# Side steps of a first MLP map tied to the emptying of a PSUM bank

## The chip, the cores and the metric

The kernel runs on one core of a Trainium2 chip, in one launch. The metric is device time in microseconds (us) from start to end of the execution. The engines are TensorE (PE for matmuls, PEld for its weight loads), VectorE (DVE), ScalarE (ACT), GpSimd (POOL) and SyncE (SP); each works through its own instructions in a fixed order and waits on semaphores for the others. DMA transfers are issued from the queues of SP and POOL.

## What is computed

One decoder layer over 2048 tokens of width 1024, in float32. `c` modulates both halves.

```python
mod = (silu(c) @ w_ada + b_ada)[:, None, :]
sh1, sc1, g1, sh2, sc2, g2 = jnp.split(mod, 6, axis=-1)
h = x * (1.0 + sc1) + sh1
z = h @ w_in                              # 1024 -> 2048
gate_b, gate_c, v_conv, v_pool = jnp.split(z, [512, 1024, 1536], axis=-1)
y_conv = gate_b * _short_conv(gate_c * v_conv, conv_w)
y_pool = _multiscale_pool(v_pool, w_pool, pool_scale)
mix = jnp.concatenate([y_conv, y_pool], axis=-1) @ w_out
x = _layer_norm(ALPHA * x + (1.0 + g1) * mix, ln1_g, ln1_b)
h = x * (1.0 + sc2) + sh2
f = jnp.square(jax.nn.relu(h @ w_mlp_in)) @ w_mlp_out   # 1024 -> 4096 -> 1024
x = _layer_norm(ALPHA * x + (1.0 + g2) * f, ln2_g, ln2_b)
```

## The kernel before

Every float32 operand of a matmul is split into a high part (an ACT copy, L135) and a low part (a DVE subtraction, L136; both in `split`), and a product is made of three matmuls (`mm3`, L140 to L142: high x high, high x low, low x high). The large maps use a scheme of seven block products in place of eight (as Strassen and Winograd have it), so sums and differences of blocks of the weights and of the activations are needed; most are made by DVE (`tt`, L145), stored to DRAM by POOL and loaded again by SP.

The tokens are worked in two blocks `b` of 1024. For each, `first_map` makes the first MLP map (1024 to 4096) in eight groups `up(b, g, ...)` of 512 columns. A group is seven products from `seven`, each of 24 matmuls into two PSUM banks. The weights of a product come from one of two generators. `summed_weights` loads blocks and sums ready from DRAM (block 1, and the first two groups of block 0; L599). `block_weights` (groups 2 to 7 of block 0) loads four blocks (L567), makes the sums on DVE (tiles `r`, L145), and stores them for block 1 (L577). Pools bound how far ahead this runs: `w` holds six tiles (three products of a high and a low part), `r` five, `o` is shared by results and side work.

After a product its two banks are emptied: by `keep` (two ACT copies, L1039), by `add` in `join` (two DVE adds, L145) or, for the last product of a group, by two ACT Relus (L1124). Relu and square of the joined results follow on ACT (L1051, L1052, L1125), and `sums` makes the block sums of the results for the second map (DVE L145, POOL stores L1064).

Beside the products, `beside` takes one step of a generator of side work, once the first groups are through: 48 steps in each block. In block 0 it is `first_side`: four steps of modulation vectors (loads L265), steps of `sum_down`, four steps `sum_x` (loads of xT at L647, an ACT affine at L648, DVE sums), two halves of `sum_weights` (loads L587), and more of `sum_down`. In block 1 it is `sum_down` alone; what is left of it runs in the second map. A step of `sum_down` makes up to two sums of blocks of the second map's weights on DVE (128x512), stores them by POOL (L1140) and issues up to three loads for the steps after it on SP (L1142), into halves of three tiles that are used over and over. So a load waits until its half has been read or stored, and an add of a later step waits for the load.

A scheduler orders the instructions of each engine by their dependencies and by priorities that follow the order in the program. Before, the dictionary `mark` held the latest weight split or bank add on DVE and the latest weight load on SP, and `beside` let every instruction of a step on those engines stand behind them, as an order within the same engine, with no wait for another engine:

```python
def beside():
    if open_:
        with tc.issue_after(mark["DVE"]), tc.issue_after(mark["SP"]):
            next(side, None)
```

Of the kernel before, what the change touches and what calls it, by code (L numbers as in the profile page):

```python
# [1 line left out]

# [8 lines left out]
AF = mybir.ActivationFunctionType  # L11
ALU = mybir.AluOpType
# [85 lines left out]
def tile_hybrid_layer(ctx: ExitStack, tc: tile.TileContext, opening, xT, x, wada, win,  # L98
                      wins, wpool, wout, wmix, w1, w2, rows, out):
    nc = tc.nc  # L100
# [11 lines left out]
    def mk(p, shape, dt, tag, bufs):  # L112
        names[0] += 1
        return p.tile(shape, dt, name=f"{tag}_{names[0]}", tag=tag, bufs=bufs)
# [7 lines left out]
    def t_w(dt=F32R):  # L122
        return mk(big, [P, T], dt, "w", 6)
# [10 lines left out]
    def split(src, hi, lo):  # L134
        high = nc.scalar.copy(hi, src)  # L135
        return high.ins, nc.vector.tensor_tensor(lo, src, hi.bitcast(F32), op=ALU.subtract).ins  # L136
# [7 lines left out]
    def tt(out_, a, b_, op):  # L144
        return nc.vector.tensor_tensor(out_, a, b_, op=op)  # L145
# [54 lines left out]
    def row_of(dst, cols):  # L200
        banks = spread(cols)
        for h, hs in enumerate(halves):
            nc.scalar.copy(dst[:, hs], banks[h])
# [58 lines left out]
    def ada(f0, f1, load=nc.gpsimd.dma_start, tiles=lambda: t_h(F32)):  # L262
        for f in range(f0, f1):
            r = tiles()
            load(r, wada[f - G1])  # L265
            dot(f, r)
        biased(f0, f1)
# [61 lines left out]
    def parts(src, t=t_h):  # L329
        hi, lo = t(), t()  # L330
        split(src, hi, lo)
        return hi, lo
# [207 lines left out]
    def beside(j, m, g1):  # L540
        for what in plan.get((j, m), "").split():
            n = int(what[1:])
            if what[0] == "r":
                ada(n, n + 2)
            elif what[0] == "f":
                fold(n, g1)
            elif what[0] == "b":
                row_of(g1, mod[:, G1 : G1 + KD])
            elif what[0] == "l":
                fold_weights(n)  # L550
            elif what[0] == "g":
                gated(n // 2, n % 2, g1)
            elif what[0] == "s":
                sum_out(n, t_o)
            else:
                sum_weights(w1[n], w1sum[n], t_o)

    mark = {}  # L560
    RAW = range(4)
    ORDER = (("11", "11"), ("12", "21"), ("s2", "2"), ("s1", "1"), ("s3", "3"), ("s4", "22"), ("22", "4"))

    def block_weights(src, dst=None):
        a11, a12, a21, a22 = [t_r() for _ in range(4)]
        for i, r in enumerate((a11, a12, a21, a22)):
            mark["SP"] = nc.sync.dma_start(r, src[i]).ins  # L567
        yield a11
        yield a12
        s1 = t_r()  # L570
        tt(s1, a21, a22, ALU.add)
        tt(a21, a11, a21, ALU.subtract)
        tt(a11, s1, a11, ALU.subtract)
        tt(a12, a12, a11, ALU.subtract)
        if dst is not None:
            for i, r in enumerate((s1, a11, a21, a12)):
                nc.gpsimd.dma_start(dst[i], r)  # L577
        for r in (a11, s1, a21, a12, a22):
            yield r
# [16 lines left out]
    def summed_weights(src, sums, order):  # L596
        for i in order:
            r = t_r()
            mark["SP"] = nc.sync.dma_start(r, src[i] if i in RAW else sums[i - 4]).ins  # L599
            yield r  # L600

    def seven(ready, B, first_w=None):
        made = [first_w] if first_w else []

        def product(i, banks, new):
            if made:
                hi, lo = made.pop()
            else:
                r = next(ready)
                hi, lo = t_w(), t_w()  # L610
                mark["DVE"] = split(r, hi, lo)[1]
            for p in range(2):
                if new:
                    banks[p] = t_ps()
                for k in range(4):
                    bh, bl = B[ORDER[i][1], k // 2]
                    ks = slice((k % 2) * H, (k % 2) * H + H)
                    cs = slice(p * H + k * P, p * H + k * P + P)
                    mm3(banks[p], hi[:, cs], lo[:, cs], bh[:, ks], bl[:, ks], new and k == 0, k == 3,
                        not new)  # L620

        return product
# [403 lines left out]
    def sum_out(g, tiles):  # L1026
        sum_blocks([gout[i % 2, i // 2 * 2 + g] for i in range(4)], wosum[g], tiles)

    def up(b, g, B, beside, turn):
        X, Y, Z = {}, {}, {}  # L1030
        order = (0, 1, 5, 4, 6, 7, 3) if g else (0, 1, 7, 4, 5, 6, 3)
        product = seven(summed_weights(w1[g], w1sum[g], order) if b or g < 2 else block_weights(w1[g], w1sum[g]), B)
        ps = [slice(p * H, p * H + H) for p in range(2)]
        parts_, where, spare = {}, {}, []

        def keep(banks):
            r = t_o()
            for p in range(2):
                nc.scalar.copy(r[:, ps[p]], banks[p])  # L1039
            return r  # L1040

        def add(r, banks):
            for p in range(2):
                mark["DVE"] = tt(r[:, ps[p]], r[:, ps[p]], banks[p], ALU.add).ins

        def join(r, banks):
            add(r, banks)
            squared(r)

        def squared(r):  # L1050
            nc.scalar.activation(r, r, AF.Relu)  # L1051
            nc.scalar.activation(r, r, AF.Square)  # L1052

        def cell(r, i):
            return r[:, i * Q : i * Q + Q]

        def made(r, fh, th):
            for q in range(2):
                for f in range(2):
                    i = 4 * (2 * th + q) + 2 * fh + f  # L1060
                    parts_[i] = where[i] = cell(r, 2 * f + q)

        def stored(slot, z):
            nc.gpsimd.dma_start(usum[slot, g // 2, :, b, g % 2, :], z)  # L1064

        def sums(stage):
            if stage == 0:
                stored(RAW_SLOT[0], parts_[RAW_SLOT[1]])
            for x, y, sign, slot, at in U_SUMS[stage]:
                if at not in parts_:  # L1070
                    r = t_o()
                    parts_.update({16 + 4 * len(spare) + i: cell(r, i) for i in range(4)})
                    spare.append(r)
                z = parts_[at]
                tt(z, where[x], where[y], ALU.add if sign > 0 else ALU.subtract)
                where[16 + sum(k > 15 for k in where)] = z
                if slot >= 0:
                    stored(slot, z)

        product(0, X, True)  # L1080
        c11 = keep(X)
        beside()
        product(1, Y, True)
        join(c11, Y)
        made(c11, 0, 0)
        sums(0)
        beside()
        yield
        if g == 0:
            product(5, Y, True)  # L1090
            yield
            product(3, Z, True)
            c22 = keep(Z)
            yield
        product(2, X, False)
        c12 = keep(X)
        if g == 0:
            add(c12, Y)
            join(c12, Z)
            yield  # L1100
        else:
            beside()
            product(3, Z, True)
            c22 = keep(Z)
            beside()
        product(4, X, False)
        join(c22, X)
        made(c22, 1, 1)
        sums(1)
        beside()  # L1110
        if g == 0:
            yield
        else:
            if g == NC - 1:
                turn()
            product(5, Z, False)
            join(c12, Z)
            beside()
        made(c12, 0, 1)
        sums(2)  # L1120
        product(6, X, False)
        c21 = t_o()
        for p in range(2):
            nc.scalar.activation(c21[:, ps[p]], X[p], AF.Relu)  # L1124
        nc.scalar.activation(c21, c21, AF.Square)  # L1125
        made(c21, 1, 0)
        sums(3)
        beside()


    def sum_down():
# [247 lines left out]
    def first_map(b, B, back):  # L1379
        side = sums_down if b else first_side()  # L1380
        open_ = []

        def beside():
            if open_:
                with tc.issue_after(mark["DVE"]), tc.issue_after(mark["SP"]):
                    next(side, None)

        def turn():
            if b + 1 < NB:
                ready.append(prepare())  # L1390

        ups = [up(b, g, B, beside, turn) for g in range(NC)]
        for g in range(2):
            next(ups[g])
            back(1 + g)
        for i in range(3, 7):
            next(ups[0])
            back(i)
        open_.append(True)
        for g in range(NC):  # L1400
            for _ in ups[g]:
                pass

    ready = []
# [60 lines left out]
```

## Time and profile before

| what | value |
|---|---|
| median of 3 runs | 1855.06 us (1849.86 to 1859.36) |
| the profiled execution | 1847.54 us, its span 1845.5 us |
| PE, DVE, ACT, POOL busy | 1723.2, 1416.8, 842.6, 402.4 us |
| mean granted TensorE clock | 0.969 |
| DMA | 478.95 MB, mean 260 GB/s |

The profile shows one execution. Its groups of instructions name the line, the engine, the operation and the tiles (output <- inputs). A wait is put down to what ended it. In the timeline a row has its start, its duration, and in brackets the idle time just before it with what released it. The first map of block 0 with its side steps lies at about 380 to 660 us of the span, that of block 1 at about 945 to 1250 us.

### The profile page before, as it was taken

Reading aid. Unit: us, or ns where it says so; the run is one execution under the profiler, and the core shown is the slowest. Engines: PE = TensorE matmul, PEld = TensorE weight load, DVE = VectorE, ACT = ScalarE, POOL = GpSimd, SP = SyncE. Lnnn points to the kernel's source line nnn. Section 1 sums busy time; section 2 is a strip of 40 time slices with the busy share of each in tenths; the row PEclk is TensorE's granted clock in tenths of the full one; section 3 lists DMA queues with packets and bytes.
Section 4 is the critical chain, followed back from the end, with each engine's and each line's share of the span. In section 5 each row is a group of like instructions: output and inputs, shape, how many; then the busy total and the mean of one; then the engine's idle time right before and its main releaser. Section 6 shows DMA issues by size and latency. Waiting matters only on the chain.

```text
span 1845.5 us, 22577 instructions
## 1 busy us (share of the span) xinstructions
PE 1723.2 (93%) x7519; PEld 1414.0 (77%) x7519; DVE 1416.8 (77%) x2222; ACT 842.6 (46%) x1148; POOL 402.4 (22%) x767
## 2 busy tenths in 40 slices
PE   9999998777969789999988999998999999999998
PEld 8888886656747678888866877876888888888887
DVE  7997886687777776689676787777675586686998
ACT  6322475344434374344754444454544334353552
POOL 0223121244454430010113455443000000000000
PEclk9999999888989999999998999999999999999999
DMA  9998764588987874257546888889977787666772
GB/s 388 349 338 321 301 247 161 189 289 283 327 290 278 285 249 151 98 189 261 181 162 224 283 291 292 292 281 353 370 273 250 254 285 284 221 246 219 268 277 80
DMA packets 155205, 478.95 MB, mean 260 GB/s; under 512 B 22600, under 2 KB 23120, under 8 KB 155088
## 3 DMA queue, kind: packets, MB, share of 16 engines
q1 hardware_dynamic: 100960, 304.44, 47.8%
q0 software_dynamic: 54128, 173.07, 26.0%
q8 instruction: 59, 0.97, 0.2%
q14 instruction: 58, 0.48, 0.1%
HBM read 315.40 MB, written 162.01 MB: 259 GB/s over the span
## 4 chain that ended last, share of the span: by engine, by line
PE 48%; DMA 10%; DVE 9%; issue 5%; POOL 2%; ACT 1%; SPq 0%; DVEq 0%; POOLq 0%; ACTq 0%
PE ps L142 16%; PE ps L141 16%; PE ps L140 16%; DVE o L145 6%; DMA o<-in_w 3%; DMA wsum<-o 3%; DMA usum<-o 2%; DVE w L136 2%; POOL usum L1064 1%; DMA r<-in_w 1%; DMA r<-winsum 1%; DVE h L136 0%; DMA o<-hsave 0%; DMA o<-in_xT 0%; POOL wsum L1140 0%
## 5 line engine op out<-in xcount | busy, mean ns | idle before, releaser
L140 PE MATMUL ps<-h,w 128*128 128x512 f32 x1312 | 522.4, 399 | 61.9 <-ACT w L135 39.1
L142 PE MATMUL ps<-h,w 128*128 128x512 f32 x1312 | 521.5, 399 | 34.3 <-DVE w L136 34.2
L141 PE MATMUL ps<-h,w 128*128 128x512 f32 x1312 | 521.2, 397 | 9.3 <-DVE h L136 9.3
L141 PE MATMUL ps<-h,h 128*128 128x512 f32 (+1 forms) x1064 | 413.3, 388 | 6.2 <-DVE h L136 6.2
L142 PE MATMUL ps<-h,h 128*128 128x512 f32 (+1 forms) x1064 | 413.2, 388 | 0.0
L140 PE MATMUL ps<-h,h 128*128 128x512 f32 (+1 forms) x1064 | 412.3, 388 | 0.0
L140 PEld LDWEIGHTS ps<-h,w 128*128 128x128 f32 x1312 | 252.4, 193 | 119.6 <-ACT w L135 41.2
L142 PEld LDWEIGHTS ps<-h,w 128*128 128x128 f32 x1312 | 252.7, 193 | 94.2 <-DVE w L136 41.4
L145 DVE TENSOR_TENSOR o<-o,o 128x256 f32<-128x256 f32 (+2 forms) x554 | 265.6, 527 | 55.0 <-DMA o<-in_w 23.1
L141 PEld LDWEIGHTS ps<-h,w 128*128 128x128 f32 x1312 | 252.9, 193 | 65.7 <-DVE h L136 12.0
L1064 POOL DMA_DIRECT2D usum<-o x416 | 222.9, 541 | 232.6 <-DVE o L145 173.3
L135 ACT CAST w<-r 128x1024 fp32r<-128x1024 f32 x156 | 163.5, 1051 | 228.5 <-PE ps L141 210.1
L135 ACT CAST h<-r 128x1024 fp32r<-128x1024 f32 (+1 forms) x144 | 144.8, 1011 | 235.5 <-PE ps L141 121.0
L141 PEld LDWEIGHTS ps<-h,h 128*128 128x128 f32 x1064 | 200.3, 188 | 48.0 <-DVE h L136 7.1
L136 DVE TENSOR_TENSOR w<-r,w 128x1024 fp32r<-128x1024 f32 x156 | 190.4, 1223 | 58.7 <-ACT w L135 58.3
L140 PEld LDWEIGHTS ps<-h,h 128*128 128x128 f32 x1064 | 200.1, 188 | 41.2 <-DVE o L944 0.2
L142 PEld LDWEIGHTS ps<-h,h 128*128 128x128 f32 x1064 | 200.2, 188 | 40.8
L136 DVE TENSOR_TENSOR h<-r,h 128x1024 fp32r<-128x1024 f32 (+1 forms) x144 | 167.6, 1171 | 64.4 <-ACT h L135 64.0
L145 DVE TENSOR_TENSOR o<-o 128x256 f32<-128x256 f32 (+1 forms) x240 | 125.3, 530 | 73.9 <-DMA o<-in_w 48.5
L145 DVE TENSOR_TENSOR o<-o,ps 128x512 f32<-128x512 f32 x172 | 113.8, 685 | 30.0 <-PE ps L142 27.8
L136 DVE TENSOR_TENSOR h<-w,h 128x1024 fp32r<-128x1024 f32 x104 | 127.0, 1221 | 6.9 <-ACT h L135 6.8
L135 ACT CAST h<-w 128x1024 fp32r<-128x1024 f32 x104 | 108.8, 1046 | 18.2 <-DVE w L145 9.7
(163 smaller groups left out, 1350.2 us busy)
## 6 DMA issues: line engine op xcount, KB each, us to landing
usum<-o POOLq DMA_DIRECT2D x416, 128.0 KB, 4.8
r<-usum SPq DMA_DIRECT2D x104, 512.0 KB, 5.2
wsum<-o POOLq DMA_DIRECT2D x136, 256.0 KB, 4.9
w<-wsum SPq DMA_DIRECT2D x68, 512.0 KB, 5.3
r<-in_w SPq DMA_DIRECT2D x54, 512.0 KB, 5.6
o<-in_w SPq DMA_DIRECT2D x104, 256.0 KB, 4.9
r<-w1sum SPq DMA_DIRECT2D x40, 512.0 KB, 5.3
w<-in_w SPq DMA_DIRECT2D x36, 512.0 KB, 6.1
```

Of the source, the lines that this page charges most:

```text
L135: high = nc.scalar.copy(hi, src)
L136: return high.ins, nc.vector.tensor_tensor(lo, src, hi.bitcast(F32), op=ALU.subtract).ins
L140: nc.tensor.matmul(ps, whi, xhi, start=first, stop=False, skip_group_check=goes_on)
L141: nc.tensor.matmul(ps, whi, xlo, start=False, stop=False, skip_group_check=goes_on)
L142: nc.tensor.matmul(ps, wlo, xhi, start=False, stop=last, skip_group_check=goes_on)
L145: return nc.vector.tensor_tensor(out_, a, b_, op=op)
L1064: nc.gpsimd.dma_start(usum[slot, g // 2, :, b, g % 2, :], z)
```

## The change

Each product now leaves in `mark` the instruction that empties its second bank: the ACT copy of `keep`, the DVE add of `add`, or the ACT Relu of the last product. `beside` gets this instruction, and `behind` adds to every DVE and SP instruction that the step traces a dependency on it. On the same engine it is an order; across engines it is a wait on a semaphore. So a load on SP always waits for ACT or DVE, and an add on DVE waits for ACT after a `keep` or a Relu. Instructions of a step on ACT and POOL get no such dependency. The old marks go: a step no longer has to stand behind the latest weight split on DVE or the latest weight load on SP. The steps, their loads and their sums are the same.

```diff
-    mark = {}
+    @contextmanager
+    def behind(ins):
+        traced = nc.cur_bb.bb.instructions
+        n = len(traced)
+        yield
+        for i in traced[n:]:
+            if i.engine in (nc.vector.engine, nc.sync.engine):
+                tc.add_manual_dep(i, ins.name, mybir.DependencyInfo(
+                    mybir.DependencyClass.NoSync if i.engine == ins.engine else mybir.DependencyClass.Sync,
+                    mybir.DependencyReason.DATA), reason="behind")
...
-            mark["SP"] = nc.sync.dma_start(r, src[i]).ins
+            nc.sync.dma_start(r, src[i])
...
-            if made:
-                hi, lo = made.pop()
-            else:
-                r = next(ready)
-                hi, lo = t_w(), t_w()
-                mark["DVE"] = split(r, hi, lo)[1]
+            hi, lo = made.pop() if made else parts(next(ready), t_w)
...
     def up(b, g, B, beside, turn):
-        X, Y, Z = {}, {}, {}
+        X, Y, Z, mark = {}, {}, {}, [None]
...
         def keep(banks):
             r = t_o()
             for p in range(2):
-                nc.scalar.copy(r[:, ps[p]], banks[p])
+                mark[0] = nc.scalar.copy(r[:, ps[p]], banks[p]).ins
             return r
 
         def add(r, banks):
             for p in range(2):
-                mark["DVE"] = tt(r[:, ps[p]], r[:, ps[p]], banks[p], ALU.add).ins
+                mark[0] = tt(r[:, ps[p]], r[:, ps[p]], banks[p], ALU.add).ins
...
-        beside()
+        beside(mark[0])
...
         for p in range(2):
-            nc.scalar.activation(c21[:, ps[p]], X[p], AF.Relu)
+            mark[0] = nc.scalar.activation(c21[:, ps[p]], X[p], AF.Relu).ins
...
-        def beside():
+        def beside(ins):
             if open_:
-                with tc.issue_after(mark["DVE"]), tc.issue_after(mark["SP"]):
+                with behind(ins):
                     next(side, None)
```

All seven calls of `beside` in `up` are changed in this way, and `summed_weights` like `block_weights`. `parts`, which was there already, makes the two tiles, splits into them and returns them.

More of the change, by code (lines that the diff above doesn't have):

```diff
@@ L1 @@
-from contextlib import ExitStack, nullcontext
+from contextlib import ExitStack, contextmanager, nullcontext
 import concourse.bass as bass
@@ L598, in summed_weights @@
             r = t_r()
-            mark["SP"] = nc.sync.dma_start(r, src[i] if i in RAW else sums[i - 4]).ins
+            nc.sync.dma_start(r, src[i] if i in RAW else sums[i - 4])
             yield r
@@ L1086, in up @@
         sums(0)
-        beside()
+        beside(mark[0])
         yield
@@ L1101, in up @@
         else:
-            beside()
+            beside(mark[0])
             product(3, Z, True)
             c22 = keep(Z)
-            beside()
+            beside(mark[0])
         product(4, X, False)
@@ L1109, in up @@
         sums(1)
-        beside()
+        beside(mark[0])
         if g == 0:
@@ L1117, in up @@
             join(c12, Z)
-            beside()
+            beside(mark[0])
         made(c12, 0, 1)
@@ L1127, in up @@
         sums(3)
-        beside()
+        beside(mark[0])
     def sum_down():
```

## The prediction

> **What bounds the kernel now.** I read the page first, for the engine that sets the time.
>
> ```profile
> span 1845.5 us, 22577 instructions
> PE 1723.2 (93%) x7519; PEld 1414.0 (77%) x7519; DVE 1416.8 (77%) x2222; ACT 842.6 (46%) x1148; POOL 402.4 (22%) x767
> ```
>
> PE is busy for 93% of the span. So a gain can only come from its idle stretches, and a loss only from new ones. The change acts in the first MLP map of each token block. The table of stretches puts these two maps at about 380 to 660 us and 945 to 1250 us.
>
> ```profile
> core 0: us, PE busy (x) PEld busy (x) DVE busy (x) ACT busy (x) POOL busy (x), PEclk, DMA share, GB/s
> 380.00:660.00 280.00, 226.26 (x937) 182.80 (x938) 210.47 (x368) 118.12 (x140) 128.49 (x240) 0.90 0.83 288
> 660.00:945.00 285.00, 279.62 (x1253) 230.23 (x1252) 219.92 (x315) 153.21 (x233) 32.73 (x58) 0.99 0.54 188
> 945.00:1250.00 305.00, 279.39 (x1176) 226.45 (x1175) 229.84 (x419) 138.62 (x163) 133.88 (x250) 0.96 0.82 267
> ```
>
> Without side work (660 to 945) PE idles 285 - 279.6 = 5.4 us. In the first map of block 0 it idles 280 - 226.3 = 53.7 us, in that of block 1, 305 - 279.4 = 25.6 us. DVE has 210 of 280 us of work there, and the DMA engines are 82 to 83% busy. The view of waits names what PE waits for (line, what ended the wait, total, times, longest), first for 380 to 660, then for 945 to 1250.
>
> ```profile
> PE ps L140 <- ACT w L135: 38.2, 4, 18.1
> PE ps L142 <- DVE w L136: 18.7, 6, 5.2
> DVE o L145 <- DMA o<-in_w: 22.0, 6, 5.6
> ```
>
> ```profile
> PE ps L142 <- DVE w L136: 11.3, 4, 4.7
> DVE o L145 <- DMA o<-in_w: 37.8, 12, 7.3
> ```
>
> In block 0 PE waits for weights: the high half (ACT cast, L135) or the low half (DVE subtraction, L136). Behind both stand the sums of the weight blocks and the side steps, all on DVE in one fixed order. The side steps themselves wait for loads.
>
> **The change: what is held.** No instruction is added or removed; the costs are those of order and of new waits. Before, a step's DVE adds (L145) and SP loads (L1142, L587, L647) only had to stand behind the latest weight split or bank add, and the latest weight load. After, each waits until the bank of the product beside it is empty. Matched with its bank's emptying (I call that the mark), 73 of 114 side loads and 57 of 174 side adds of the trace started before it; 13 loads more than 10 us before. The others lose nothing. Two such cases, loads of a step at 464 to 467 us and the ends of the bank adds they will wait for (ACT starts right behind these):
>
> ```profile
> 464.05 1.34 SPq L1142 DMA_DIRECT2D o<-in_w  x3
> 465.70 1.63 SPq L647 DMA_DIRECT2D o<-in_xT  x2
> 472.78 1.06 ACT L1051 ACTIVATE o<-o 128x1024 f32<-128x1024 f32 x1 [0.86 <-DVE o L145]
> 478.72 1.06 ACT L1051 ACTIVATE o<-o 128x1024 f32<-128x1024 f32 x1 [1.35 <-DVE o L145]
> ```
>
> The three loads go 472.8 - 464.1 = 8.7 us later, the two of xT 478.7 - 465.7 = 13.0 us. Behind a held load stand on SP the weight loads of the group (L567, L599); behind a held add stand on DVE the bank adds and weight splits, and for these PE waits. POOL's stores of sums follow their adds. A load, once issued, lands as this row says:
>
> ```profile
> o<-in_w SPq DMA_DIRECT2D x104, 256.0 KB, 4.9
> ```
>
> The new order has a second effect, in block 0. The static order shows the four block sums (r<-r,r, L145, 5.00 us) of a group and its first splits standing 27 to 62 places earlier on DVE. Thus weights can be ready earlier.
>
> **Stall by stall.** These are the starts of PE after its long idles, with the idle and its releaser in brackets:
>
> ```profile
> 386.14 0.80 PE L140 MATMUL ps<-h,w 128*128 128x512 f32 x1 [9.25 <-ACT w L135]
> 390.42 0.79 PE L142 MATMUL ps<-h,w 128*128 128x512 f32 x1 [3.48 <-DVE w L136]
> 453.71 0.80 PE L142 MATMUL ps<-h,w 128*128 128x512 f32 x1 [3.00 <-DVE w L136]
> 552.27 0.80 PE L140 MATMUL ps<-h,w 128*128 128x512 f32 x1 [18.12 <-ACT w L135]
> 595.43 0.50 PE L142 MATMUL ps<-h,w 128*128 128x512 f32 x1 [2.39 <-DVE w L136]
> 602.98 0.50 PE L142 MATMUL ps<-h,w 128*128 128x512 f32 x1 [1.81 <-DVE w L136]
> 646.77 0.80 PE L142 MATMUL ps<-h,w 128*128 128x512 f32 x1 [5.24 <-DVE w L136]
> 1030.70 0.50 PE L142 MATMUL ps<-h,w 128*128 128x512 f32 x1 [1.10 <-DVE w L136]
> 1154.36 0.79 PE L142 MATMUL ps<-h,w 128*128 128x512 f32 x1 [4.70 <-DVE w L136]
> 1209.39 0.50 PE L142 MATMUL ps<-h,w 128*128 128x512 f32 x1 [2.95 <-DVE w L136]
> ```
>
> ```profile
> 389.14 1.22 DVE L136 TENSOR_TENSOR w<-r,w 128x1024 fp32r<-128x1024 f32 x1
> 393.29 5.00 DVE L145 TENSOR_TENSOR r<-r,r 128x1024 f32<-128x1024 f32 x4
> ```
>
> At 386 and 390 PE had stood since 386.14 - 9.25 = 376.9. In the new order the split of 389.14 stands 34 places earlier, that of the next product 28, and the four sums lie ahead of the side adds. The 9.25 + 3.48 = 12.7 us go. Late next is the third product: two run from 376.9 to about 387.8 (24 matmuls of about 0.227 us each), and its low half stands behind side adds whose load now waits for the mark and for an add before it, issued near 388.5. It lands 4.9 us later, at 393.4; an add (0.6), a block sum (1.2) and the split (1.2) end near 396.5. A stall of 8.7 us stays: 8.7 - 12.7 = -4.0.
>
> At 453 the block sum moves behind a bank add and a step's xT loads behind their mark; I get a restart near 450.6, or -3.1 in all: +1.0.
>
> At 496 the held loads of the rows at 464.05 and 465.70 feed DVE and the ACT affine (L648), which stands ahead of the next Relu on ACT. I take the rest of the shift as given back: +3.1.
>
> At 552 the high half is ready by about 528, since its block sums stand 36 to 39 places earlier, but the low half is not. Two steps that DVE had done in its slack now wait for the Relu copy and the next keep (L1124, L1039):
>
> ```profile
> 509.01 0.69 DVE L145 TENSOR_TENSOR o<-o 128x512 f32<-128x512 f32 x1
> 525.00 1.29 DVE L145 TENSOR_TENSOR o<-o 128x512 f32<-128x512 f32 x2
> 539.29 1.08 ACT L1124 ACTIVATE o<-ps 128x512 f32<-128x512 f32 x2 [12.01 <-DMA winsum<-o]
> 543.87 1.07 ACT L1039 COPY o<-ps 128x512 f32<-128x512 f32 x2 [2.40 <-DMA usum<-o]
> 552.86 1.23 DVE L136 TENSOR_TENSOR w<-r,w 128x1024 fp32r<-128x1024 f32 x1
> ```
>
> Their adds now come near 546 to 548, the second step's load is issued behind the first's add at 548.1 and lands at 553.0; five ops of 0.34 to 0.60 us (2.7) and the split (1.2) end at 556.9, against 552.86 + 1.23 = 554.1. The 18 us stall stays, +2.8.
>
> At 595 and 602 the splits now stand ahead of a waiting side add: 2.39 + 1.81 = 4.2 go, -4.2. At 646 the high half comes earlier, the low half not: -0.2 beyond the shift.
>
> In block 1 the weights are loaded ready summed, three products (16 us) ahead, which hides most holds of 2 to 10 us. At 1030 I find the low half 2.2 us later, for two loads that go 5.7 us later, at the next keep: +2.2. At 1209 the split moves ahead of the side adds, of which the first had waited 4.29 us for its load: -2.9. The stall of 1154 stays, as does the start of the second map. The rows are these loads, those adds and that split:
>
> ```profile
> 993.93 0.91 SPq L1142 DMA_DIRECT2D o<-in_w  x2
> 1205.04 1.29 DVE L145 TENSOR_TENSOR o<-o,o 128x512 f32<-128x512 f32 x2 [4.29 <-DMA o<-in_w]
> 1208.12 1.22 DVE L136 TENSOR_TENSOR w<-r,w 128x1024 fp32r<-128x1024 f32 x1
> ```
>
> **Clock.** After a long idle PE runs slowly, and a longer idle may cost more than itself:
>
> ```profile
> 395.28 0.63 PE L140 MATMUL ps<-h,w 128*128 128x512 f32 x1
> 395.70 0.47 PE L141 MATMUL ps<-h,w 128*128 128x512 f32 x1
> 396.24 0.39 PE L140 MATMUL ps<-h,w 128*128 128x512 f32 x1
> 396.46 0.39 PE L141 MATMUL ps<-h,w 128*128 128x512 f32 x1
> ```
>
> From 390.42 to 395.70 matmuls start 0.42 us apart, then about 0.22: 5.3 us at half rate, 2.6 us lost. The restart takes 0.79 to 0.80 us after 3.00 idle (behind an earlier idle), 4.70 and more, 0.50 after 2.95 and less. I count the same four slow restarts in block 0 before and after, so this term is 0. The Trainium skill, "TensorE: Matmul & The Clock Gate", Part 1, says that an idle window of some 3.4 us halves the clock and that about 3.4 us of work restores it. By it a slow restart would cost 1.7 us where the trace has 2.6, and the sum would be the same.
>
> **Sum.** Block 0: -4.0 + 1.0 + 3.1 + 2.8 - 4.2 - 0.2 = -1.5. Block 1: 2.2 - 2.9 = -0.7. Together -2.2 us on the profiled execution, which took 1847.5 us (span 1845.5) and lies 7.5 us below the median of 1855.06. On the median this gives 1853. Each term is uncertain by one load (4.9 us) either way, because an order made for one set of times meets another; eight such terms, if independent, make 4.9 x 2.8 = 14 us.
>
> **Rivals.** Slower: the steps bunch at the ends of groups. The Relu mark and the keep of the next group lie close together when ACT is held up (539.29 and 543.87 above), so steps that had run apart follow one another, each with add, load, add; DVE stands at the second add for 4.9 us, with the bank adds and splits behind it. For it: the DVE waits for in_w (37.8 us in block 1), 77% DVE load. Against: 41 loads were late already, and block 1 has 16 us of cushion. It decides from the point where the held load lands after the low half is due. At five group ends of block 0 that is 5 x 4.9 = 24.5 us, less the 4.2 that go at 595: +20, 1875.
>
> Faster: the earlier block sums decide. If the side loads land in time after all, the waits for the cast shrink by half: 38.2 / 2 = 19, with two slow restarts less, 5.2: -24, 1831. For it: the order moves the sums by up to 62 places. Against: at 552 the low half is behind the same adds.
>
> Nothing happens, since 117 of 174 adds were behind their marks already: 1855.
>
> **How the numbers follow.** My sum gets 0.46, nothing 0.06, bunching 0.28, the earlier sums 0.20. About 0.5% (9 us) is what a measurement of this kernel can tell from no change. My sum's -2 with a spread of 14 us lies beyond -9 in about 3 of 10 cases and beyond +9 in 2 of 10. So faster is 0.20 + 0.46 x 0.3 = 0.33, slower 0.28 + 0.46 x 0.2 = 0.38, and the same has the rest, 0.29. Cases of both signs hold most of the chance; the likeliest has its own range, 1853 plus or minus 18 for 8 in 10. The whole reaches over both rivals' values, with 4 us beyond the slower one for block 1, where a hold could break the cushion once: 1831 to 1879.
>
> **What would show it.** In 380 to 660 the wait of PE for the cast should fall to under 20 us, and that for the low half rise above 30, with the restart after 534 us still near 555. The first stall should end near 396. DVE's waits for in_w should grow in block 0. If the PE idle of 380 to 660 falls below 35 us, the faster rival was right; if it exceeds 70 us, or block 1 idles over 35, the slower one.

## The result and the profile after

The changed kernel is slower: 1866.77 us against 1854.61 us of the kernel before (medians of 14 runs each), a ratio of 1.0071 with a 95% interval of 1.0054 to 1.0088. Run once more beside other kernels it had a ratio of 1.0041 (1.0025 to 1.0056). So the loss is 0.4 to 0.7%, some 8 to 13 us; the forecast was 1853 us, 2 us less than before, with chances of 0.33 for faster, 0.29 for the same and 0.38 for slower.

The page and the stretches of the changed kernel. Its lines are shifted: L1147 is the load that was L1142, L1044 the copy of `keep`, L653 the affine, L652 the load of xT.

```profile
span 1864.4 us, 22605 instructions
PE 1731.2 (93%) x7519; PEld 1418.0 (76%) x7519; DVE 1417.9 (76%) x2222; ACT 841.7 (45%) x1148; POOL 403.9 (22%) x767
380.00:660.00 280.00, 227.07 (x940) 183.52 (x939) 216.49 (x389) 116.45 (x137) 132.75 (x247) 0.91 0.84 286
945.00:1250.00 305.00, 275.23 (x1158) 222.27 (x1157) 224.81 (x410) 135.85 (x159) 127.50 (x238) 0.96 0.78 254
```

PE runs the same 7519 matmuls, but is busy for 1731.2 us in place of 1723.2; the rest of the 18.9 us by which the span grew is idle time. The two stretches are the same times as before, not quite the same work: in that of block 0 the idle time is about as before (52.9 for 53.7 us), in that of block 1 it grows from 25.6 to 29.8 us, with 18 matmuls fewer done. So neither the faster rival's sign (less than 35 us idle in block 0) nor the slower one's (over 70, or over 35 in block 1) came. The waits of PE in 380 to 660 us, and then in 945 to 1250 us:

```profile
PE ps L142 <- DVE w L136: 25.0, 6, 7.0
PE ps L140 <- ACT w L135: 21.4, 2, 11.2
PE ps L140 <- ACT o L1044: 6.5, 1, 6.5
DVE o L145 <- DMA o<-in_w: 25.8, 6, 8.2
```

```profile
DVE o L145 <- DMA o<-in_w: 41.9, 16, 5.4
PE ps L142 <- DVE w L136: 14.1, 5, 5.5
```

The waits for the high half (the cast) fell from 38.2 to 21.4 us; with the new order alone (the first experiment) they are 19.8 us, so it is the order, with its earlier block sums, that lowers them. The waits for the low half rose from 18.7 to 25.0 us and from 11.3 to 14.1 us, and DVE waits more for its loads in both maps. The starts of PE after long idles, of the changed kernel:

```profile
405.00 0.80 PE L140 MATMUL ps<-h,w 128*128 128x512 f32 x1 [10.21 <-ACT w L135]
505.29 0.80 PE L142 MATMUL ps<-h,w 128*128 128x512 f32 x1 [7.01 <-DVE w L136]
550.96 0.79 PE L140 MATMUL ps<-h,w 128*128 128x512 f32 x1 [6.50 <-ACT o L1044]
559.66 0.80 PE L142 MATMUL ps<-h,w 128*128 128x512 f32 x1 [6.20 <-DVE w L136]
1044.40 0.68 PE L142 MATMUL ps<-h,w 128*128 128x512 f32 x1 [4.21 <-DVE w L136]
1292.31 0.80 PE L141 MATMUL ps<-h,h 128*128 128x512 f32 x1 [7.75 <-DVE h L136]
```

The 18.12 us stall at 552 has become two of 6.50 and 6.20. That of 1.10 at 1031 has become 4.21, and this one of the kernel before has become the 7.01 at 505:

```profile
496.49 0.50 PE L142 MATMUL ps<-h,w 128*128 128x512 f32 x1 [2.77 <-DVE w L136]
```

### The profile page after: what moved, and what is told of

It reads as the page before. It is cut to its first block, busy times and chain, and to the rows that moved or that the text cites. A ratio compares the mean times of both kernels' runs of the same rounds, so it can differ in the third digit from the quotient of the medians.

```text
span 1864.4 us, 22605 instructions
## 1 busy us (share of the span) xinstructions
PE 1731.2 (93%) x7519; PEld 1418.0 (76%) x7519; DVE 1417.9 (76%) x2222; ACT 841.7 (45%) x1148; POOL 403.9 (22%) x767
## 4 chain that ended last, share of the span: by engine, by line
PE 52%; issue 17%; DMA 14%; DVE 11%; POOL 3%; ACT 2%; SPq 0%; DVEq 0%; POOLq 0%; ACTq 0%
PE ps L141 16%; PE ps L142 16%; PE ps L140 16%; DVE o L145 7%; DMA wsum<-o 3%; DMA o<-in_w 3%; DMA usum<-o 2%; PE ps L470 2%; DVE w L136 2%; POOL usum L1069 2%; DMA o<-hsave 1%; POOL wsum L1145 1%; DVE h L136 1%; DMA o<-in_xT 1%; DVE r L145 1%
## 5 line engine op out<-in xcount | busy, mean ns | idle before, releaser
L1145 POOL DMA_DIRECT2D wsum<-o x136 | 73.7, 542 | 197.6 <-DVE o L145 188.1
```

The lines of the kernel that those rows point to most:

```text
L1145: nc.gpsimd.dma_start(wsum[i - 8, g // 2][:, cs], regs[to])
```

## The experiments

The change does two things at once: it gives DVE and SP another order, and it adds waits. The two theories were W, that the waits cost (a held load lands late and DVE stands at its add), and O, that the new order costs.

**The order without the waits.** After all is traced, the kernel lays the changed kernel's order on every engine by edges that set an order only; the dependencies of `behind` are left out. `ISSUED` holds, for each engine, the numbers of its instructions in that order. In this and the other cuts of code, `...` stands for lines left out.

```diff
-        for i in traced[n:]:
-            if i.engine in (nc.vector.engine, nc.sync.engine):
...
+    for runs in ISSUED.values():
...
+                    tc.add_manual_dep(i, last.name, mybir.DependencyInfo(
+                        mybir.DependencyClass.NoSync, mybir.DependencyReason.DATA), reason="as issued")
```

> The changed kernel's order of instructions on every engine, written out, without the waits on the bank's emptying (37 waits fewer on SP, 14 fewer on DVE). Theory W (the waits hold back loads, and DVE stands at the adds behind them): most of the loss goes, 1855 to 1858 us. Theory O (the new order is what costs, since a side add that stands late on DVE cannot run early, wait or no wait): as the changed kernel, 1863 to 1870.

Measured: 1845.53 us against 1847.21, ratio 0.9989 (0.9977 to 1.0002). The whole loss is gone, with every engine in the changed kernel's order. Theory O falls for this order; the waits cost.

**One kind held, each in the order that follows.** `behind` ties only the loads, or only the adds; the other kind keeps the old mark. `HOW` has a pair for each block, adds first; shown are the loads only, and the adds only have `('bank', 'was')` twice.

```diff
+    HOW = [('was', 'bank'), ('was', 'bank')]
...
+            if i.engine == nc.vector.engine:
+                how, was = adds, old["DVE"]
+            elif i.engine == nc.sync.engine:
+                how, was = loads, old["SP"]
...
+            to = ins if how in ("bank", "order") else was
```

> Only the SP loads of a step wait for the bank; its DVE adds stand behind the latest split or bank add as before. Theory W: the loss comes with the loads, 1864 to 1872, since the adds stand early on DVE and wait there for late loads. Theory O: the loads cost little, 1852 to 1860, and the loss comes with the adds.

> Only the DVE adds of a step wait for the bank; its SP loads stand behind the latest weight load as before. Theory W: loads come in time, 1850 to 1858. Theory O: the adds stand late and close together ahead of the weight splits, 1862 to 1870.

Measured: loads only 1.0064 (1.0046 to 1.0082), adds only 1.0048 (1.0030 to 1.0066). Neither theory had both. The scheduler gives each of them an order of its own, so these two runs, and the next, mix order and waits; the ones behind it don't.

**Block 0 alone**: `HOW` has `('bank', 'bank')` for block 0 and `('was', 'was')`, the old marks, for block 1:

> The change in block 0 alone; block 1 as before. Seen from the trace, PE is late by about 3 us at the end of the first map of block 0 (663 us) and by 9 to 10 us when that of block 1 begins, and by 14 to 17 us when it ends. Both theories: the change in block 0 costs 5 to 10 us, so 1860 to 1865. If it were block 1 alone that pays: 1853 to 1857.

Measured: 1.0020 (1.0009 to 1.0032), 1851.71 us against 1847.21: 3.7 us by the ratio and 4.5 by the medians, a little under the 5 to 10 that were expected. Again the order is another one.

**The changed kernel's order with a part of its waits.** From here on all kernels but one have the changed kernel's order, written out as in the first, and differ in the waits alone. Shown is the edit for SP; the others have `(nc.vector.engine,)`, or both engines with `b in (0,)` or `b in (1,)`.

```diff
-            if i.engine in (nc.vector.engine, nc.sync.engine):
+            if b in (0, 1) and i.engine in (nc.sync.engine,):
```

> The changed kernel's order on every engine, with the added waits on SP alone (the loads); the 14 on DVE left out. If held loads are the cause (theory L): 0.5 to 0.8% above the kernel before, as the changed kernel. If DVE's own waits for ACT are (theory D): as the order alone, within 0.2% of the kernel before.

> The changed kernel's order on every engine, with the added waits on DVE alone (14); the loads are free. Theory L: within 0.2% of the kernel before. Theory D: 0.5 to 0.8% above it. If each pays at places of its own, both this one and the one with SP's waits lie between.

> The changed kernel's order, with all added waits of block 0 and none of block 1. Against the order alone, the changed kernel's trace loses 4.2 and 5.7 us at two products of block 0 (near 402 and 500 us) and 2 elsewhere there, so 9 to 12 us are expected above the order alone, 0.4 to 0.6% above the kernel before.

> The changed kernel's order, with all added waits of block 1 and none of block 0. Against the order alone the changed kernel's trace loses 5.7 us at a product near 1033 us and 3.0 near 1112 and gets 1.5 back, so 5 to 8 us are expected above the order alone, 0.2 to 0.4% above the kernel before.

Measured: SP alone 1.0044 (1.0021 to 1.0067), DVE alone 0.9982 (0.9965 to 0.9998), block 0 alone 1.0028 (1.0010 to 1.0046), block 1 alone 1.0000 (0.9985 to 1.0015). The held loads are the cause, though at a little less than the 0.5 to 0.8% expected; DVE's own waits for ACT cost nothing that could be measured. Block 0 paid less than expected, 3.9 thousandths above the order alone (the 0.9989 of the first experiment) for an expected 5 to 6.5, and block 1 1.1 for 2.7 to 4.3.

**The changed kernel again.**

> The changed kernel once more, to stand beside the others of this call. Its first ratio was 1.0071; with the waits on SP alone it was 1.0044, on DVE alone 0.9982, with the order alone 0.9989. If the two kinds of waits add up, 1.003 to 1.006; if they need each other, 1.006 to 1.009.

Measured: 1855.27 us against 1847.51, 1.0041 (1.0025 to 1.0056), as with the waits on SP alone. In its profile (the second profile of the changed kernel) the span is 1853.5 us. Three places show the mechanism. These are SP's queue and DVE near 500 us, in this run of the changed kernel, and then PE's restart:

```profile
475.90 1.28 SPq L1147 DMA_DIRECT2D o<-in_w  x3
481.85 1.66 SPq L652 DMA_DIRECT2D o<-in_xT  x2
491.09 0.69 DVE L145 TENSOR_TENSOR o<-o 128x512 f32<-128x512 f32 x1 [3.52 <-ACT o L653]
493.69 1.63 DVE L145 TENSOR_TENSOR o<-o,o 128x512 f32<-128x512 f32 x3 [1.57 <-ACT o L653]
503.13 1.22 DVE L136 TENSOR_TENSOR w<-r,w 128x1024 fp32r<-128x1024 f32 x1
504.40 0.79 PE L142 MATMUL ps<-h,w 128*128 128x512 f32 x1 [7.33 <-DVE w L136]
```

The same instructions with the order alone (its lines: load L1399, xT L904, split L395):

```profile
463.65 1.33 SPq L1399 DMA_DIRECT2D o<-in_w  x3
469.59 3.96 SPq L904 DMA_DIRECT2D o<-in_xT  x2
484.75 0.69 DVE L404 TENSOR_TENSOR o<-o 128x512 f32<-128x512 f32 x1
495.16 1.23 DVE L395 TENSOR_TENSOR w<-r,w 128x1024 fp32r<-128x1024 f32 x1
496.44 0.50 PE L401 MATMUL ps<-h,w 128*128 128x512 f32 x1 [2.10 <-DVE w L395]
```

Held, the xT loads go at 481.85 in place of 469.59; DVE, in its fixed order, stands for 3.52 and 1.57 us until the affine behind them is done; the split ends 8.0 us later and PE idles 7.33 us in place of 2.10. (PE as a whole was 2.7 us behind the order alone by then; the other 5.2 us are the longer idle.)

The second place is in block 1, near 1033 us: a step's first three loads wait for the Relu copy (L1129) that ends at 1000 us. DVE stands at the adds that need them, 1.42 and 1.59 us, and then 3.25 us at an add whose load waits on SP for the store of an earlier sum (changed kernel, then the order alone):

```profile
1000.12 1.28 SPq L1147 DMA_DIRECT2D o<-in_w  x3
1006.47 1.03 DVE L145 TENSOR_TENSOR o<-o,o 128x512 f32<-128x512 f32 x2 [1.42 <-DMA o<-in_w]
1009.09 0.69 DVE L145 TENSOR_TENSOR o<-o,o 128x512 f32<-128x512 f32 x1 [1.59 <-DMA o<-in_w]
1016.57 1.03 DVE L145 TENSOR_TENSOR o<-o 128x512 f32<-128x512 f32 x2 [3.25 <-DMA o<-in_w]
1033.93 1.22 DVE L136 TENSOR_TENSOR w<-r,w 128x1024 fp32r<-128x1024 f32 x1
1035.20 0.79 PE L142 MATMUL ps<-h,w 128*128 128x512 f32 x1 [3.92 <-DVE w L136]
```

```profile
990.10 1.38 SPq L1399 DMA_DIRECT2D o<-in_w  x3
1010.19 1.03 DVE L404 TENSOR_TENSOR o<-o 128x512 f32<-128x512 f32 x2 [1.11 <-DMA o<-in_w]
1027.63 1.22 DVE L395 TENSOR_TENSOR w<-r,w 128x1024 fp32r<-128x1024 f32 x1
```

With the order alone PE's trace shows no idle there. The third place is the stall near 402 us, whose loads lie further ahead: those of the modulation vectors (`in_wada`) go 12.7 us later, and DVE stands at them (changed kernel, then the order alone):

```profile
362.11 17.06 SPq L265 DMA_DIRECT2D o<-in_wada  x8
376.51 1.22 DVE L256 SCALAR_TENSOR_TENSOR o<-o,o 128x1024 f32<-128x1024 f32 x1 [3.66 <-DMA o<-in_wada]
403.97 0.79 PE L140 MATMUL ps<-h,w 128*128 128x512 f32 x1 [9.80 <-ACT w L135]
```

```profile
349.42 27.46 SPq L524 DMA_DIRECT2D o<-in_wada  x8
373.21 1.22 DVE L515 SCALAR_TENSOR_TENSOR o<-o,o 128x1024 f32<-128x1024 f32 x1 [0.57 <-DMA o<-in_wada]
401.69 0.79 PE L399 MATMUL ps<-h,w 128*128 128x512 f32 x1 [5.94 <-ACT w L394]
```

**One product of lead for the loads**, in the same order, no added waits on DVE:

```diff
-            if i.engine in (nc.vector.engine, nc.sync.engine):
+            if i.engine == nc.sync.engine:
...
+            marks.append(ins)
             if open_:
-                with behind(ins):
+                with behind(marks[-2]):
```

> The changed kernel's order; the loads of a step wait for the bank of the product before the one beside them, some 5.4 us earlier; no added waits on DVE. If the held loads cost because they land after the add that needs them stands first on DVE (a load takes 4.9 us), one product of lead brings all back: within 0.2% of the kernel before. If any tie of SP to the banks costs: 0.3 to 0.5% above it.

Measured: 1.0004 (0.9992 to 1.0016). A tie of SP to the banks costs nothing against the kernel before if it leaves the load its landing time; the 1.5 thousandths above the order alone lie within the two intervals. Its xT loads of that step and its restart of PE:

```profile
472.39 1.61 SPq L911 DMA_DIRECT2D o<-in_xT  x2
495.66 0.50 PE L401 MATMUL ps<-h,w 128*128 128x512 f32 x1 [2.11 <-DVE w L395]
```

**Only the xT loads held:**

```diff
-            if i.engine in (nc.vector.engine, nc.sync.engine):
+            if i.engine == nc.sync.engine and i.name in held:
...
+            held.add(nc.sync.dma_start(r, xT[i]).ins.name)
```

> The changed kernel's order; of all added waits only those of the eight xT loads in block 0 (steps of the sums of x) are left. The loss of 5.7 to 6.1 us at the product that restarts near 508 us in the changed kernel should be here, the one near 402 us not: 0.2 to 0.35% above the order alone, 0.1 to 0.25% above the kernel before. If the site needs the other held loads too: as the order alone.

Measured: 0.9981 (0.9969 to 0.9993). A miss: the stall of that product did grow, from 2.10 to 4.77 us, but about half as far as with all loads held (7.33), and the time did not rise.

```profile
474.80 1.39 SPq L913 DMA_DIRECT2D o<-in_xT  x2
494.79 0.79 PE L401 MATMUL ps<-h,w 128*128 128x512 f32 x1 [4.77 <-DVE w L395]
```

**The order of the adds-only kernel without its waits**, written out in the same way:

> The order on every engine of the kernel in which the adds alone were held (it was 0.48% above the kernel before), without its 13 waits on DVE. If those waits cost there: within 0.2% of the kernel before. If that order costs by itself: 0.3 to 0.6% above it.

Measured: 1.0034 (1.0023 to 1.0046). Most of the 0.48% of that kernel is its order. So an order can cost as much as the waits; the changed kernel's does not.

**The held loads in two parts**, the loads of eight steps, and (with `not in`) those of all others:

```diff
+    SITES = 5, 6, 17, 18, 19, 48, 49, 50
...
-            if i.engine in (nc.vector.engine, nc.sync.engine):
+            if i.engine == nc.sync.engine and (step in SITES):
```

> The changed kernel's order; added waits on SP alone, and only for the loads of eight steps: 5 and 6, 17 to 19 (block 0) and 48 to 50 (block 1), which lie ahead of the products near 402, 500 and 1033 us where the traces of the held loads lose 4 to 6 us each. If these are the cause: as all waits on SP, 0.3 to 0.5% above the kernel before. If the loss is spread over many loads: within 0.15% of the kernel before.

> The changed kernel's order; added waits on SP alone, for the loads of all steps but those eight. If those eight are the cause: as the order alone, 0 to 0.2% below the kernel before. If the loss is spread: 0.2 to 0.5% above it.

Measured: the eight steps alone 1.0065 (1.0046 to 1.0083), all others 1.0025 (1.0013 to 1.0037). The eight are enough for a loss as large as that of the whole change; the others, expected free, cost some too. Both ran beside a kernel before of 1854.05 us, so they are to be set against the 1.0071 of the first comparison (1854.61 us); the order alone was not run there. The eight steps bring 4 of the added waits that the traces hold on SP, the others 32. The starts of PE at the three places, with the eight steps and then with the others:

```profile
399.95 0.79 PE L399 MATMUL ps<-h,w 128*128 128x512 f32 x1 [6.44 <-ACT w L394]
502.13 0.80 PE L401 MATMUL ps<-h,w 128*128 128x512 f32 x1 [6.45 <-DVE w L395]
1039.60 0.80 PE L401 MATMUL ps<-h,w 128*128 128x512 f32 x1 [4.34 <-DVE w L395]
```

```profile
403.30 0.80 PE L399 MATMUL ps<-h,w 128*128 128x512 f32 x1 [9.86 <-ACT w L394]
498.96 0.50 PE L401 MATMUL ps<-h,w 128*128 128x512 f32 x1 [2.11 <-DVE w L395]
1033.34 0.50 PE L401 MATMUL ps<-h,w 128*128 128x512 f32 x1 [1.49 <-DVE w L395]
```

So the eight steps hold two of the places. The third, near 402, belongs to the others, against what was expected: with the eight it idles about as with the order alone (5.94), with the others as in the changed kernel (9.80). The two losses add up to more than the whole change's; what a stall at one place changes behind it stays open.

## Why the prediction was wrong

PE's matmuls can be counted through, so the n-th of one trace can be set beside the n-th of another. The table shows by how much PE fell behind the kernel before in each stretch (times of the trace before), in the second profile of the changed kernel and with the order alone. The two profiles of the changed kernel differ by up to 3 us in a stretch, so smaller numbers say nothing. The rows are rounded one by one.

| stretch | forecast | changed | order alone |
|---|---|---|---|
| up to 376 us | none | +6.4 | +8.0 |
| 386 and 390 | -4.0 | -3.3 | -7.5 |
| 453 | +1.0 | +0.3 | +0.1 |
| 496 | +3.1 | +6.1 | -0.7 |
| 552 (510 to 575) | +2.8 | -5.4 | -3.7 |
| 595 and 602 | -4.2 | -2.7 | -0.5 |
| 646 | -0.2 | -4.1 | -4.5 |
| 655 to 700 | none | +5.9 | +6.2 |
| 700 to 1005 | none | -1.5 | +1.8 |
| 1030 | +2.2 | +5.2 | -1.0 |
| 1066 to 1170 | none | -6.6 | -6.8 |
| 1209 | -2.9 | -3.3 | -3.2 |
| 1225 to 1263 (end of block 1's first map) | none | +8.6 | +7.8 |
| 1263 to 1285 (start of the second map) | none | +2.5 | +2.8 |
| sum | -2.2 | +8.0 | -1.2 |

What was right: the places. At 386 the stall moved one product on (10.21 us in the first profile, forecast 8.7), but PE waited there for the cast, not for the low half, and the loads that held DVE were those of `in_wada`, so that 8.7 is partly luck; at 496, 1030 and 1209 the sign was as told, and at 496 the cause too, the held xT loads and the affine. The wait for the cast was forecast to fall below 20 us and fell to 21.4; that for the low half was to exceed 30 us and came to 25.0.

What failed, by its step:

- The terms of the held loads were mis-sized. At 496 I had 3.1 us, which was not a cost worked out but "the rest of the shift", taken as given back; it was 6.1, and against the order alone 6.8. At 1030 I had 2.2; it was 5.2. At 386 the hold took 4.1 us of the order's gain, -3.3 for -7.5. These three, 4.1 + 6.8 + 6.1 = 17 us against the order alone, are each of the size of a load's landing (4.9 us), where I had a rest or 2.2; 8 us of them are given back in other rows of the table.
- The clock term was put at 0, with "the same four slow restarts". It was not 0. PE was busy for 7.8 us longer in the second profile with the same 7519 matmuls, about as much as the whole +8.0 of the table; with the order alone it was 4.6 us:

```profile
PE 1731.0 (93%) x7519; PEld 1418.5 (77%) x7519; DVE 1418.6 (77%) x2222; ACT 842.0 (45%) x1148; POOL 402.9 (22%) x767
PE 1727.8 (94%) x7519; PEld 1418.1 (77%) x7519; DVE 1418.6 (77%) x2222; ACT 841.8 (46%) x1148; POOL 402.6 (22%) x767
```

  Matmuls that start 0.3 to 0.6 us after the one before number 169 in the kernel before, 208 in the second profile and 188 with the order alone. Near 1033 the 3.92 us of idle are followed by starts 0.44 us apart until 1040.06, then 0.23: some 2.4 us more, which makes up the 6.1 within 0.2.
- The stall at 552 was called unchanged, "+2.8". It shrank by 5.4 us: PE could start with the high half and then waited for a bank (6.50 us on L1044, in the first profile) and for the low half (6.20), less than the 18.12 before. The delay of two steps, which I had priced at a landing, did not show: the order alone gains 3.7 us there, the changed kernel 5.4.
- Four stretches were not in my sum: the modulation steps before 376 us (+6.4), the end of the first map of block 0 (+5.9), that of block 1 (+8.6), and the start of the second map, of which I wrote that it "stays" (+2.5). The +8.6 is one new stall at a product where the kernel before has no idle, with the slow matmuls behind it (second profile, then the order alone):

```profile
1239.60 0.79 PE L142 MATMUL ps<-h,w 128*128 128x512 f32 x1 [5.53 <-DVE w L136]
1229.70 0.80 PE L401 MATMUL ps<-h,w 128*128 128x512 f32 x1 [4.67 <-DVE w L395]
```

  All four are there with the order alone, so they are the order's; that they are balanced by 552, 646 and 1066 to 1170 (where the stall of 1154 was to stay) was not known from my walk.

So my "sum near zero" holds for the order alone (-1.2 us in the table, 0.9989 measured), and there by terms of which I had half wrong; the waits came on top. The slower rival named the mechanism (DVE stands at an add whose load is held) but put it at five group ends with 24.5 us; it was three places, and half of it came back. (The chance of slower, 0.28 + 0.46 x 0.2, is 0.37 and not 0.38.) The faster rival was right about the cast's waits and wrong about their worth: the low half took over.

What stays open: why the loss was 0.7% in the first comparison and 0.4% in the second, where the kernel before itself stood at 1854.6 and 1847.5 us. That the held loads of block 1 alone cost nothing measurable (1.0000) fits their trace: there the product near 1033 us restarts after 2.89 us of idle in 0.50 us, at full rate, and the row of 1030 would read +1.8 in place of +5.2. Why it loses less with block 0 free stays open too.

## What to carry to other kernels

A hold on a prefetch must leave it its landing time: tied to the product beside the step, a 4.9 us load landed after the add that needed it stood first on DVE; tied one product earlier, it cost nothing that could be told from the kernel before. To judge a scheduling edit, part its order from its waits by laying the new order down without them; here the order was neutral and the 37 more waits on SP were the loss, 4 of them enough for one as large. When a hand-walked sum nearly cancels, count through the stretches that were called unchanged as well: the largest term here, 8.6 us, was at a product that had no stall before.

## What was not expected of the hardware

Waits of DVE on ACT, 14 more of them, cost nothing that could be measured (0.9982). Two orders of the same instructions without any added wait differed by 0.45% (0.9989 and 1.0034), more than half of the whole change.
